# Gate and up products of a mixture of experts: eight of 512 columns, then eight of 256, in place of eight pairs

## The chip, the cores and the metric

The kernel runs on one core of one Trainium2 chip. The metric is the time of one execution on the device in microseconds (us), the median of several runs. A core has five engines that work side by side: TensorE (PE) multiplies matrices, VectorE (DVE) and ScalarE (ACT) work elementwise, GpSimd (POOL) here issues gathers and scatters, SyncE (SP) issues DMA transfers. TensorE loads a stationary operand of up to 128 x 128 (the "weights" of a product, a row PEld LDWEIGHTS in the profile) and streams a moving operand of up to 512 columns past it (a row PE MATMUL); the result goes to PSUM, where further products may be added.

## The reference

One layer of a bidirectional encoder over 2,048 tokens of 1,024 channels: a mixer stage (long convolution, neighbourhood attention, pooling), and behind it a mixture of 16 experts, each of which takes the 256 tokens that score highest for it. The change lies in the experts:

```python
def expert_choice_moe(h, w_router, w_gate, w_up, w_down):
    ...
    aff = jax.nn.softmax(h.astype(F32) @ w_router.astype(F32), axis=-1)
    gate, idx = lax.top_k(aff.transpose(0, 2, 1), cap)
    xs = jax.vmap(lambda hb, ib: hb[ib])(h, idx)
    a = jnp.einsum('becd,edf->becf', xs, w_gate)
    b = jnp.einsum('becd,edf->becf', xs, w_up)
    y = jnp.einsum('becf,efd->becd', jax.nn.silu(a) * b, w_down)
    y = y * gate.astype(y.dtype)[..., None]
    ...
```

Each expert has 1,024 x 2,048 weights for gate and for up and 2,048 x 1,024 for down, in float32.

## The kernel before

Products are made in a rounded float32 format (fp32r). To keep the precision, each operand is split into a high part, rounded, and a low part, the rest. `split` (L210 to L213) does it: ScalarE casts the high part (L212), VectorE subtracts it from the original (L213). A product of two split operands is then three products: high by high, high by low, low by high.

For an expert, `lookahead` gathers its 256 tokens (two gathers of 128 rows, tiles mo_xg, L1210), transposes them on TensorE (L1226, sixteen transposes into banks tp) and splits them into the tile mo_xx: eight slices d of 128 channels, and in each the high parts of 256 tokens beside their low parts, 512 columns in one row. It runs for the next expert in the middle of the present one (f = 3). VectorE also copies the gate's values out of the gathered rows (L1230, tile mo_gt) and builds the next indices from sums over mo_oh (L1193).

`experts` runs over 16 experts. The gate and up stage has eight steps f of 256 hidden channels, and in each a block for gate and one for up. A block loads 1 MB of weights (SP, mo_raw), splits it into mo_wh and mo_wl (three buffers each), and multiplies for two halves m of 128 hidden channels and eight slices d. For each d there is a pair: the high weights by all 512 columns of the tokens, high and low at once (L1257, tile mo_wh, 512 columns), and the low weights by the high tokens alone (L1259, tile mo_wl, 256 columns), which is added to the second half of the bank. ScalarE copies that half out (L1261), VectorE adds the other (L1262), and Silu and a product (L1265, L1266) and a split make mo_hh and mo_hl. There are 16 blocks of 32 products in an expert, 8 pairs for each m. Behind them come the down products, 192 for an expert, all of 512 columns, by `mm3` (L228, L229, L230).

The same `mm3` makes the products of the earlier stages that are cited later: the projection (tiles w_h, w_l, hT_h, hT_l, of 512 columns, and of 256 for the values) and the filter's transforms (t, d2p, of 256 columns).

A scheduler of the framework sets the order of each engine's instructions from the dependencies and an estimate of times when the program is built; within its rules the loops' order is kept for products that add to one bank. TensorE, VectorE and ScalarE each work through their list in order.

Of the kernel before, what the change touches and what calls it, by code (L numbers as in the profile page):

```python
# [183 lines left out]
class Trunk:  # L184
# [8 lines left out]
    def sb(self, pool, shape, tag, dt=F, bufs=None):  # L193
        kw = {} if bufs is None else {"bufs": bufs}
        return pool.tile(list(shape), dt, tag=tag, name=self.name(tag), **kw)
# [949 lines left out]
    def experts(self, pool):  # L1145
# [20 lines left out]
        def weights(src):  # L1166
            raw = sb(list(src.shape), "mo_raw", F, 3)
            nc.sync.dma_start(raw, src)
            h = sb(list(src.shape), "mo_wh", R, 3)
            l = sb(list(src.shape), "mo_wl", R, 3)  # L1170
            self.split(h, l, raw)
            return h, l
# [42 lines left out]
        def lookahead(e):  # L1215

            idx, xg = tokens(e)
            gate = sb([128, 2], "mo_gt", F, 2)
            xx = sb([128, 8, 2, 256], "mo_xx", R, 2)
            xh, xl = xx[:, :, 0], xx[:, :, 1]  # L1220
            for h in range(2):
                for q in range(2):
                    pt = self.bank("tp", (128, 4, 128))
                    for d in range(4):
                        dd = q * 4 + d
                        nc.tensor.transpose(pt[:, d, :], xg[h][:, dd * 128:(dd + 1) * 128], self.ident)  # L1226
                    sl = (slice(None), slice(q * 4, q * 4 + 4), slice(h * 128, h * 128 + 128))
                    self.split(xh[sl], xl[sl], pt)
                    self.first = nc.cur_bb.bb.instructions[-1]
                nc.vector.tensor_copy(gate[:, h:h + 1], xg[h][:, D + e:D + e + 1])  # L1230
            return idx, gate, xx
# [6 lines left out]
        for e in range(NE):  # L1238
            idx, gate, xx = nxt
            hh = sb([128, 16, 256], "mo_hh", R, 1)  # L1240
            hl = sb([128, 16, 256], "mo_hl", R, 1)
            for f in range(8):
                if e == 0 and f == 1:
                    late.close()
                    late.enter_context(self.tc.issue_after(first))
                if e == 1 and f == 0:
                    late.close()
                acc = []
                for src in (wg, wu):
                    w, wlo = weights(src[e, :, :, f * 256:f * 256 + 256])  # L1250


                    pt = self.bank("mm", (128, 2, 2, 256))
                    for m in range(2):
                        ms = slice(m * 128, m * 128 + 128)
                        for d in range(8):
                            nc.tensor.matmul(pt[:, m].rearrange("p k t -> p (k t)"), lhsT=w[:, d, ms],  # L1257
                                             rhs=xx[:, d].rearrange("p k t -> p (k t)"), start=d == 0, stop=False)
                            nc.tensor.matmul(pt[:, m, 1], lhsT=wlo[:, d, ms], rhs=xx[:, d, 0], start=False, stop=d == 7)  # L1259
                    a = sb([128, 2, 256], "mo_s", F, 3)  # L1260
                    nc.scalar.activation(a, pt[:, :, 1], AF.Copy)  # L1261
                    nc.vector.tensor_tensor(a, a, pt[:, :, 0], op=OP.add)  # L1262
                    acc.append(a)
                s = acc[0]
                nc.scalar.activation(s, s, AF.Silu)  # L1265
                nc.vector.tensor_tensor(s, s, acc[1], op=OP.mult)  # L1266
                self.split(hh[:, f * 2:f * 2 + 2], hl[:, f * 2:f * 2 + 2], s)
                if f == 3 and e + 1 < NE:
                    nxt = lookahead(e + 1)
            pair = [self.bank("mm", (128, 2, 512)) for h in range(2)]  # L1270
            po = [[pair[h][:, n] for n in range(2)] for h in range(2)]
            for u in range(8):
                w, wlo = weights(wd[e, :, u * 2:u * 2 + 2, :])
                for h in range(2):
                    for n in range(2):
                        for d in range(2):
                            dd = u * 2 + d
                            ts = slice(h * 128, h * 128 + 128)
                            ns = slice(n * 512, n * 512 + 512)
                            self.mm3(po[h][n], hh[:, dd, ts], hl[:, dd, ts], w[:, d, ns], wlo[:, d, ns], dd == 0, dd == 15)  # L1280
            last = e == NE - 1
            if last:
                self.final_all(pool, gf, out)
            for h in range(2):
                off = bass.IndirectOffsetOnAxis(ap=idx[:, h:h + 1].bitcast(U32), axis=0)
                y = sb([128, D], "mo_y", F, 2)
                if not last:
                    for n in range(2):
                        nc.scalar.activation(y[:, n * 512:n * 512 + 512], po[h][n], AF.Copy, scale=gate[:, h:h + 1])  # L1289
                    nc.gpsimd.indirect_dma_start(out=self.Acc, out_offset=off, in_=y, in_offset=None, compute_op=OP.add)  # L1290
                else:
                    xa = sb([128, D], "mo_xa", F, 2)
                    nc.gpsimd.indirect_dma_start(out=xa, out_offset=None, in_=self.Acc, in_offset=off)
                    for n in range(2):
                        ns = slice(n * 512, n * 512 + 512)
                        nc.vector.scalar_tensor_tensor(xa[:, ns], po[h][n], gate[:, h:h + 1], xa[:, ns],
                                                       op0=OP.mult, op1=OP.add)
                    self.final_norm(pool, y, xa, gf)
                    nc.gpsimd.indirect_dma_start(out=out, out_offset=off, in_=y, in_offset=None)
# [198 lines left out]
```

## Time and profile before

| | us |
|---|---|
| median of 3 runs | 3329.43 |
| lowest and highest run | 3318.08, 3336.1 |
| the profiled execution | 3334.13 |
| its span, first to last instruction | 3332.3 |
| TensorE, products | 3187.5 (96% of the span) |
| VectorE | 1968.4 (59%) |
| ScalarE | 1543.7 (46%) |
| GpSimd | 369.2 (11%) |

Busy time is the time in which at least one instruction of an engine runs. Products on TensorE overlap: the next starts while the one before drains, so the recorded duration of one is longer than the step to the next. The time that a stream of products takes is read from their starts. The experts run from 1147.9 us to the end, 2,184 of the 3,332 us.

A row of grouped instructions gives line, engine, operation, written tile <- read tiles, shapes and count, then busy time and mean duration in ns, then idle time of the engine just before them and who ended it. A row of the timeline gives start, duration, engine, line and operation, and in brackets the idle time before it with its releaser.

### The profile page before, as it was taken

Reading aid. Unit: us, or ns where it says so; the run is one execution under the profiler, and the core shown is the slowest. Engines: PE = TensorE matmul, PEld = TensorE weight load, DVE = VectorE, ACT = ScalarE, POOL = GpSimd, SP = SyncE. Lnnn points to the kernel's source line nnn. Section 1 sums busy time; section 2 is a strip of 40 time slices with the busy share of each in tenths; the row PEclk is TensorE's granted clock in tenths of the full one; section 3 lists DMA queues with packets and bytes.
Section 4 is the critical chain, followed back from the end, with each engine's and each line's share of the span. In section 5 each row is a group of like instructions: output and inputs, shape, how many; then the busy total and the mean of one; then the engine's idle time right before and its main releaser. Section 6 shows DMA issues by size and latency. Waiting matters only on the chain.

```text
span 3332.3 us, 44701 instructions
## 1 busy us (share of the span) xinstructions
PE 3187.5 (96%) x17646; PEld 2685.8 (81%) x17646; DVE 1968.4 (59%) x2684; ACT 1543.7 (46%) x2068; POOL 369.2 (11%) x472
## 2 busy tenths in 40 slices
PE   7999996998999499999999999999999999999998
PEld 5878885776788388888888888888888888888886
DVE  5244485445676775665655756657566566565665
ACT  4243332556432354454554545545445455454464
POOL 2222122212111000000000000000000000000012
PEclk9999998999899699999999999999999999999999
DMA  9557898567454366566676666766666667666596
GB/s 287 185 180 255 266 337 233 175 213 205 140 170 144 123 202 202 197 208 203 202 207 194 206 202 202 208 204 195 209 196 209 204 195 215 195 195 202 194 303 227
DMA packets 431144, 690.22 MB, mean 207 GB/s; under 512 B 28034, under 2 KB 325746, under 8 KB 430678
## 3 DMA queue, kind: packets, MB, share of 16 engines
q1 hardware_dynamic: 370326, 534.99, 50.6%
q0 software_dynamic: 31472, 107.09, 11.0%
q10 hardware_dynamic: 29136, 45.29, 3.9%
q8 instruction: 139, 2.28, 0.3%
q14 instruction: 71, 0.58, 0.1%
HBM read 578.58 MB, written 119.03 MB: 209 GB/s over the span
## 4 chain that ended last, share of the span: by engine, by line
PE 87%; DMA 6%; issue 2%; DVE 2%; ACT 1%; POOL 1%; SPq 1%; POOLq 0%; ACTq 0%; DVEq 0%
PE mm L1257 27%; PE mm L1259 14%; PE mm L228 11%; PE mm L229 11%; PE mm L230 11%; PE mm L217 3%; PE o L217 1%; PE tp L217 1%; PE s L217 1%; PE tp L1226 1%; DMA at_t<-Ce 1%; DMA wo_raw<-in_w_out 1%; DMA mo_xg<-Hr,mo_ix 1%; DMA x<-in_x 1%; DMA at_k<-KD 0%
## 5 line engine op out<-in xcount | busy, mean ns | idle before, releaser
L1257 PE MATMUL mm<-mo_xx,mo_wh 128*128 128x512 f32 x4096 | 1442.7, 397 | 0.8 <-DVE mo_xx L213 0.6
L213 DVE TENSOR_TENSOR mo_wl<-mo_raw,mo_wh 128x2048 fp32r<-128x2048 f32 x384 | 879.8, 2291 | 757.5 <-ACT mo_wh L212 757.3
L1259 PE MATMUL mm<-mo_xx,mo_wl 128*128 128x256 f32 x4096 | 1148.8, 281 | 0.0
L212 ACT ACTIVATE mo_wh<-mo_raw 128x2048 fp32r<-128x2048 f32 x384 | 735.8, 1917 | 713.4 <-PE mm L230 317.6
L1257 PEld LDWEIGHTS mm<-mo_xx,mo_wh 128*128 128x128 f32 x4096 | 769.6, 188 | 182.9 <-DVE mo_xx L213 1.0
L1259 PEld LDWEIGHTS mm<-mo_xx,mo_wl 128*128 128x128 f32 x4096 | 774.3, 189 | 0.7
L229 PE MATMUL mm<-mo_wl,mo_hh 128*128 128x512 f32 x1024 | 398.6, 389 | 0.0
L228 PE MATMUL mm<-mo_wh,mo_hh 128*128 128x512 f32 x1024 | 398.0, 389 | 0.0
L230 PE MATMUL mm<-mo_wh,mo_hl 128*128 128x512 f32 x1024 | 396.2, 389 | 0.0
L1290 POOL DMA_INDIRECT Acc<-mo_y,mo_ix x30 | 71.8, 2394 | 1386.6 <-ACT mo_y L1289 1272.5
L228 PEld LDWEIGHTS mm<-mo_wh,mo_hh 128*128 128x128 f32 x1024 | 192.2, 188 | 40.2
L230 PEld LDWEIGHTS mm<-mo_wh,mo_hl 128*128 128x128 f32 x1024 | 192.2, 188 | 40.0
L229 PEld LDWEIGHTS mm<-mo_wl,mo_hh 128*128 128x128 f32 x1024 | 192.2, 188 | 39.6
L1262 DVE TENSOR_TENSOR mo_s<-mo_s,mm 128x512 f32<-128x512 f32 x256 | 174.2, 680 | 0.0
L1265 ACT ACTIVATE mo_s<-mo_s 128x512 f32<-128x512 f32 x128 | 80.7, 630 | 194.7 <-DVE mo_s L1262 194.7
L228 PE MATMUL mm<-hT_h,w_h 128*128 128x512 f32 x384 | 155.8, 411 | 6.0 <-ACT hT_h L212 6.0
L229 PE MATMUL mm<-hT_l,w_h 128*128 128x512 f32 x384 | 154.9, 404 | 0.0
L230 PE MATMUL mm<-hT_h,w_l 128*128 128x512 f32 x384 | 154.1, 403 | 0.0
L1261 ACT ACTIVATE mo_s<-mm 128x512 f32<-128x512 f32 x256 | 147.8, 577 | 0.0
L212 ACT ACTIVATE mo_hh<-mo_s 128x512 fp32r<-128x512 f32 x128 | 79.7, 623 | 74.5 <-DVE mo_s L1266 74.5
L816 ACT ACTIVATE at_s<-at_s,at_min 128x360 f32<-128x360 f32 (+5 forms) x128 | 76.5, 598 | 72.0 <-DVE at_min L812 67.8
L228 PE MATMUL mm<-wo_h,mx_h 128*128 128x512 f32 x256 | 104.2, 407 | 4.0 <-DVE wo_x L1026 3.6
(325 smaller groups left out, 3878.0 us busy)
## 6 DMA issues: line engine op xcount, KB each, us to landing
mo_raw<-in_w_gate SPq DMA_DIRECT2D x128, 1024.0 KB, 11.4
mo_raw<-in_w_up SPq DMA_DIRECT2D x128, 1024.0 KB, 5.3
mo_raw<-in_w_down SPq DMA_DIRECT2D x128, 1024.0 KB, 4.8
w_r<-c_w_in_t SPq DMA_DIRECT2D x60, 256.0 KB, 8.3
x<-in_x SPq DMA_DIRECT2D x24, 512.0 KB, 4.3
Ud<-e ACTq DMA_DIRECT2D x32, 256.0 KB, 6.8
Hd<-t ACTq DMA_DIRECT2D x32, 256.0 KB, 5.5
t<-Hd SPq DMA_DIRECT2D x16, 512.0 KB, 7.3
```

Of the source, the lines that this page charges most:

```text
L212: self.nc.scalar.activation(hi, src, AF.Copy)
L213: self.nc.vector.tensor_tensor(lo, src, hi.bitcast(F), op=OP.subtract)
L217: ins = op(*args, **kw).ins
L228: mm(out, lhsT=lh, rhs=rh, start=start, stop=False)
L229: mm(out, lhsT=lh, rhs=rl, start=False, stop=False)
L230: mm(out, lhsT=ll, rhs=rh, start=False, stop=stop)
L816: nc.scalar.activation(s[:, 0:nk], s[:, 0:nk], AF.Exp, bias=mins[:, y:y + 1], scale=-1.0, accum_out=w.sums[:, col:col + 1])
L1257: nc.tensor.matmul(pt[:, m].rearrange("p k t -> p (k t)"), lhsT=w[:, d, ms], rhs=xx[:, d].rearrange("p k t -> p (k t)"), start=d == 0, sto ...
L1259: nc.tensor.matmul(pt[:, m, 1], lhsT=wlo[:, d, ms], rhs=xx[:, d, 0], start=False, stop=d == 7)
L1261: nc.scalar.activation(a, pt[:, :, 1], AF.Copy)
L1262: nc.vector.tensor_tensor(a, a, pt[:, :, 0], op=OP.add)
L1265: nc.scalar.activation(s, s, AF.Silu)
```

## The change

In the gate and up block the loop over the eight slices d is split in two: for each half m, all eight products with the high weights come first, and all eight with the low weights behind them. The products, their operands and their sums into the bank are the same; the start and stop marks stay on the first and on the last.

```diff
                         for d in range(8):
                             nc.tensor.matmul(pt[:, m].rearrange("p k t -> p (k t)"), lhsT=w[:, d, ms],
                                              rhs=xx[:, d].rearrange("p k t -> p (k t)"), start=d == 0, stop=False)
+                        for d in range(8):
                             nc.tensor.matmul(pt[:, m, 1], lhsT=wlo[:, d, ms], rhs=xx[:, d, 0], start=False, stop=d == 7)
```

From the added line on, the lines of the changed kernel count one higher: L1259 becomes L1260, L1262 becomes L1263, L1266 becomes L1267.

TensorE in block 10 of the first expert, around the second eight transposes of the look-ahead (tp, from mo_xg); mm_11173 is the block's bank. Before:

```order
L1257 MATMUL mm_11173<-mo_xx_10626,mo_wh_11169 128x512
L1259 MATMUL mm_11173<-mo_xx_10626,mo_wl_11170 128x256
L1257 MATMUL mm_11173<-mo_xx_10626,mo_wh_11169 128x512
L1259 MATMUL mm_11173<-mo_xx_10626,mo_wl_11170 128x256
L1226 MATMUL tp_11064<-ident,mo_xg_2296_11045 128x128 x4
L1226 MATMUL tp_11071<-ident,mo_xg_2296_11045 128x128 x4
L1257 MATMUL mm_11173<-mo_xx_10626,mo_wh_11169 128x512
L1259 MATMUL mm_11173<-mo_xx_10626,mo_wl_11170 128x256
```

Now:

```order
L1257 MATMUL mm_11173<-mo_xx_10626,mo_wh_11169 128x512 x8
L1260 MATMUL mm_11173<-mo_xx_10626,mo_wl_11170 128x256 x8
L1257 MATMUL mm_11173<-mo_xx_10626,mo_wh_11169 128x512 x7
L1226 MATMUL tp_11064<-ident,mo_xg_2296_11045 128x128 x4
L1226 MATMUL tp_11071<-ident,mo_xg_2296_11045 128x128 x4
L1257 MATMUL mm_11173<-mo_xx_10626,mo_wh_11169 128x512
L1260 MATMUL mm_11173<-mo_xx_10626,mo_wl_11170 128x256 x8
```

The pairs are gone, and the transposes stand behind 23 products of the block, where they stood behind 28. The first eight, in block 9, stand behind 10 where they stood behind 15.

VectorE in the same look-ahead, from the sum of block 7 (mm_10971) to the splits into mo_xx. Before:

```order
L1262 TENSOR_TENSOR mo_s_11004<-mo_s_11004,mm_10971 128x512
L1193 TENSOR_TENSOR mo_oh_12035<-mo_oh_12035 128x2048
L1230 COPY mo_gt_11047<-mo_xg_2295_11043 128x1
L1230 COPY mo_gt_11047<-mo_xg_2296_11045 128x1
L1266 TENSOR_TENSOR mo_s_10962<-mo_s_10962,mo_s_11004 128x512
L213 TENSOR_TENSOR mo_wl_11212<-mo_raw_11209,mo_wh_11211 128x2048
L1193 TENSOR_TENSOR mo_oh_12035<-mo_oh_12035 128x1024
L1262 TENSOR_TENSOR mo_s_11118<-mo_s_11118,mm_11085 128x512
L213 TENSOR_TENSOR mo_hl_10658<-mo_s_10962,mo_hh_10657 128x512
L213 TENSOR_TENSOR mo_xx_11048<-tp_11049,mo_xx_11048 128x4x128
L213 TENSOR_TENSOR mo_xx_11048<-tp_11056,mo_xx_11048 128x4x128
```

Now:

```order
L1263 TENSOR_TENSOR mo_s_11004<-mo_s_11004,mm_10971 128x512
L1230 COPY mo_gt_11047<-mo_xg_2295_11043 128x1
L1230 COPY mo_gt_11047<-mo_xg_2296_11045 128x1
L1193 TENSOR_TENSOR mo_oh_12035<-mo_oh_12035 128x2048
L1267 TENSOR_TENSOR mo_s_10962<-mo_s_10962,mo_s_11004 128x512
L213 TENSOR_TENSOR mo_wl_11212<-mo_raw_11209,mo_wh_11211 128x2048
L1263 TENSOR_TENSOR mo_s_11118<-mo_s_11118,mm_11085 128x512
L1193 TENSOR_TENSOR mo_oh_12035<-mo_oh_12035 128x1024
L213 TENSOR_TENSOR mo_xx_11048<-tp_11049,mo_xx_11048 128x4x128
L213 TENSOR_TENSOR mo_xx_11048<-tp_11056,mo_xx_11048 128x4x128
L213 TENSOR_TENSOR mo_hl_10658<-mo_s_10962,mo_hh_10657 128x512
```

The two copies of the gate, which wait for the gathers, have moved ahead of the widest sum over mo_oh, and the split into mo_hl has moved behind the two into mo_xx. Beside this some down products near the end of an expert have changed places among themselves, and in the last expert some of SP's loads of weights stand ahead of stores of the output.

## Rows read from the trace of the kernel before

**Rows 1.** Groups of instructions, whole span: line, engine, count | busy, mean ns | idle

```profile
L1257 PE MATMUL mm<-mo_xx,mo_wh 128*128 128x512 f32 x4096 | 1442.7, 397 | 0.8 <-DVE mo_xx L213 0.6 <-DVE mo_s L1262 0.2
L1259 PE MATMUL mm<-mo_xx,mo_wl 128*128 128x256 f32 x4096 | 1148.8, 281 | 0.0
...
L1259 PEld LDWEIGHTS mm<-mo_xx,mo_wl 128*128 128x128 f32 x4096 | 774.3, 189 | 0.7
```

**Rows 2.** Busy time by stretch: experts 3 and 13; last the clock, DMA share, GB/s

```profile
1554.40:1689.50 135.10, 135.10 (x725) 116.10 (x724) 83.09 (x86) 67.38 (x64) 6.99 (x5) 1.00 0.65 203
2905.60:3045.80 140.20, 137.45 (x726) 117.55 (x726) 82.95 (x86) 67.41 (x64) 8.51 (x5) 0.99 0.63 196
```

**Rows 3.** L1257 in three stretches: count, durations in ns, first and last start

```profile
L1257 PE MATMUL mm<-mo_xx,mo_wh x111: 389/398/403, 1554.4 to 1593.3; 128*128 128x512 f32 x111
L1257 PE MATMUL mm<-mo_xx,mo_wh x82: 391/391/475, 1617.5 to 1645.6; 128*128 128x512 f32 x82
L1257 PE MATMUL mm<-mo_xx,mo_wh x256: 389/398/504, 3181.4 to 3272.0; 128*128 128x512 f32 x128
```

**Rows 4.** Timeline of TensorE in filter and projection, ends of runs of one width

```profile
88.52 0.28 PE L228 MATMUL mm<-w_h,hT_h 128*128 128x256 f32 x1
...
89.47 0.28 PE L230 MATMUL mm<-w_h,hT_l 128*128 128x256 f32 x1
...
218.67 0.28 PE L229 MATMUL fl<-t,d2p 128*128 128x256 f32 x1
...
219.85 0.39 PE L229 MATMUL mm<-hT_l,w_h 128*128 128x512 f32 x1
...
221.71 0.39 PE L228 MATMUL mm<-hT_h,w_h 128*128 128x512 f32 x1
...
365.65 0.40 PE L230 MATMUL mm<-hT_h,w_l 128*128 128x512 f32 x1
...
367.75 0.39 PE L230 MATMUL mm<-hT_h,w_l 128*128 128x512 f32 x1
```

**Rows 5.** TensorE into the down products (experts 2 and 14), and settled (expert 3)

```profile
1510.85 0.39 PE L228 MATMUL mm<-mo_wh,mo_hh 128*128 128x512 f32 x1
...
1512.70 0.39 PE L230 MATMUL mm<-mo_wh,mo_hl 128*128 128x512 f32 x1
...
L228 PE MATMUL mm<-mo_wh,mo_hh x61: 389/389/389, 1648.0 to 1688.8; 128*128 128x512 f32 x61
...
3137.90 0.40 PE L228 MATMUL mm<-mo_wh,mo_hh 128*128 128x512 f32 x1
...
3139.73 0.39 PE L230 MATMUL mm<-mo_wh,mo_hl 128*128 128x512 f32 x1
```

**Rows 6.** Timeline of the look-ahead in expert 3, TensorE's gate and up left out

```profile
1606.14 1.21 DVE L1193 TENSOR_TENSOR mo_oh<-mo_oh 128x2048 bf16<-128x2048 bf16 x1
1607.27 0.14 DVE L1230 COPY mo_gt<-mo_xg 128x1 f32<-128x1 f32 x1
...
1608.03 1.03 PE L1226 MATMUL tp<-ident,mo_xg 128*128 128x128 f32 x8
1608.44 0.15 DVE L1230 COPY mo_gt<-mo_xg 128x1 f32<-128x1 f32 x1 [1.02 <-DMA mo_xg<-Hr,mo_ix]
1608.51 0.68 DVE L1266 TENSOR_TENSOR mo_s<-mo_s,mo_s 128x512 f32<-128x512 f32 x1
...
1613.11 1.28 DVE L213 TENSOR_TENSOR mo_xx<-tp,mo_xx 128x512 fp32r<-128x512 f32 x2
...
1616.66 1.03 PE L1226 MATMUL tp<-ident,mo_xg 128*128 128x128 f32 x8
```

**Rows 7.** Timeline of the look-ahead in expert 13

```profile
2965.39 0.15 DVE L1230 COPY mo_gt<-mo_xg 128x1 f32<-128x1 f32 x1 [6.79 <-DMA mo_xg<-Hr,mo_ix]
...
2970.81 1.97 PE L1226 MATMUL tp<-ident,mo_xg 128*128 128x128 f32 x8 [2.75 <-DVE mo_xx L213]
```

## The prediction

> **What bounds the kernel now.** I read the groups of instructions first, with shapes kept apart. The two gate and up products are the largest: 4,096 of 512 columns (L1257) and 4,096 of 256 (L1259), with 0.8 us of idle time before all the first and none before the second [rows 1]. So in this stage TensorE waits for nothing: no product waits for its weights, although VectorE makes the low half, which L1259 needs, last. The granted clock over a whole expert is 1.00 [rows 2], its upper level, 2.4 GHz. What counts is therefore not the recorded duration of a product (397 and 281 ns), in which neighbours overlap, but the step from one start to the next. For that I took first and last starts over long stretches.
>
> The step is not one number. In the first nine of expert 3's sixteen blocks (a block is one gate or up slab of 32 products, 16 pairs), 111 starts of L1257 lie between 1554.4 and 1593.3 us: 38.9 / 110 = 353.6 ns for a pair. In its last blocks 82 starts lie between 1617.5 and 1645.6: 28.1 / 81 = 346.9 ns [rows 3]. Same instructions, same clock, same tiles; what lies between is the look-ahead, whose transposes break the stream. TensorE's stream has more than one steady rhythm and keeps the one it fell into. Experts 1 to 12 show the split of expert 3 (nine blocks and seven), expert 0 is nearly all of the quick kind, and experts 13 to 15 nearly all of the slow kind (expert 15: 90.6 / 255 = 355.3 ns with one break in it [rows 3]). That gives 12 x 9 x 16 + 3 x 256 = 2,496 slow pairs and 12 x 7 x 16 + 256 = 1,600 quick ones: a mean of 351.0 ns for a pair now.
>
> **The change part by part.** Nothing is added or taken away: 4,096 products of each kind, each with its own weight load, the same casts, evictions, loads. The multiplications are the same, so there is no saving to be had from work; there is only what the order does to the steps, to the waits, and to the instructions that the scheduler puts elsewhere.
>
> *The steps.* Seven of eight products of 512 columns now stand ahead of another of 512, and seven of eight of 256 ahead of another of 256. Both kinds of run are in the trace elsewhere, as the same fp32r products with 128 x 128 weights.
>
> For 256 behind 256: in the filter stage ten start from 218.67 to 219.85, 118.0 ns each, between products of 512 on both sides; in the projection eight steps from 88.52 to 89.47 give 118.8 [rows 4]. I take 118.3.
>
> For 512 behind 512 the trace has three answers. Right behind that run of 256 columns, eight take 219.85 to 221.71: 232.5 ns each [rows 4]. Deep in a projection run, nine take 365.65 to 367.75: 233.3 [rows 4]. Into the down products, behind the last gate and up pair, the first eight take 1510.85 to 1512.70: 231.3; but once that run has settled, 61 starts of every third product lie between 1648.0 and 1688.8, 40.8 / 60 / 3 = 226.7 ns, and when expert 14 goes into its down products, from the slow rhythm, it settles almost at once (3137.90 to 3139.73, eight steps of 228.8) [rows 5]. After the change a run of 512 is only eight long and begins behind a run of 256. The nearest rows are the two that are the first eight behind a narrower product, 232.5 and 231.3: I take 232.
>
> The pair then costs 232 + 118.3 = 350.3 ns against 351.0, and 4,096 x -0.7 ns = -2.9 us. The ends: with the quickest eight seen, 228.8 + 118.0 = 346.8, so -4.2 x 4,096 = -17 us; with runs that lock at 226.7 from the first product, 344.7, so -26 us; with the projection's 233.3 and 118.8, 352.1, so +4.5 us.
>
> Here a rule can be weighed against a row. A weight load is recorded with 189 ns [rows 1], longer than the 118 ns step of a 256-column product; today each such product has a 512 on either side, and from now on seven of eight have not. The Trainium skill, "TensorE: Matmul & The Clock Gate", section "LDWEIGHTS (loading the stationary operand)", puts a load at its columns over 1.2 GHz, which for 128 columns is an estimate of 107 ns. By that a load still fits under a product of 256 columns and the sum stays as it is; by the recorded 189 it would not, and the third rival would hold. The 118 ns steps of rows 4 agree with the page.
>
> *The waits.* The low half of the weights is needed later: the first L1259 of a slab stood one product behind the first L1257 and now stands eight behind it, 7 x 232 = 1.6 us. Since no idle time stands before L1259 [rows 1], this gives nothing; it is slack. The high half is read to the end 8 x 118 ns earlier, so ScalarE's cast into the next free buffer may start 0.9 us sooner; it waits for TensorE and not the other way round, so that is worth nothing either. The PSUM bank is complete at the same product as before.
>
> *What the scheduler moved.* In the look-ahead the first eight transposes stand ten products into block 9 where they stood fifteen, which is 8 x 232 + 2 x 118 = 2.1 us into it, against 7 x 347 + 232 = 2.7: they come 0.6 us sooner. The second eight stand 23 products into block 10 (8 x 232 + 8 x 118 + 7 x 232 = 4.4 us) where they stood 28 (14 x 350 = 4.9): 0.5 us sooner. On VectorE the two copies of the gate, which wait for the gathers, now stand ahead of the 1.21 us sum over mo_oh instead of behind it. What is queued behind them is that sum, L1266, a low half, L1262, and the splits into mo_xx that free the banks for the second transposes. In expert 3 the second gather was there at 1608.44, after a wait of 1.02 us on VectorE. From 1608.51 to 1613.11, 4.60 us, VectorE then did L1266, the low half, a step of the sum, L1262 and a split into mo_hl, and after them the two splits into mo_xx in 1.28. Now the 1.21 us go ahead of that, and the mo_hl split, which has gone behind, I leave in as a bound: 1608.44 + 0.15 + 1.21 + 4.60 + 1.28 = 1615.7 at the latest. The second transposes came at 1616.66 and will come near 1616.2 [rows 6]. Cover: 0.5 us or more, where it was 2.3; they don't wait and this part costs nothing. The first transposes came at 1608.03, and at 1607.27 the first gather was there, for the copy had no wait [rows 6]; 0.6 us sooner is 1607.4, still behind it. If the cover goes, each microsecond costs one in each expert, 15 in all.
>
> The move of a few down products by some places, and that of SP's loads of the last expert past some stores of the output, touches no engine that is waited for: TensorE has no idle time there. The start of expert 0 has the same columns at the same low clock.
>
> **The sum.** -2.9 us for the steps, nothing for the rest. The profiled execution took 3334.1 us (span 3332.3), so 3331.2; it lies 4.7 above the median of the runs shown, 3329.4, from which the same sum gives 3326.5. I forecast 3327, no change that can be told: a measurement of this kernel can tell about 0.5% from no change, which is 16.6 us (3312.8 and 3346.1).
>
> **The rivals.**
> *The runs lock.* Runs of one width settle into the quick rhythm, as the down products do, because the stream no longer changes width at each product. For it: 226.7 ns there, and the 346.9 of the quick pairs shows that gate and up can shed 7 ns too. Against it: the projection, whose weights are stationary as here, stays at 233.3 through long runs, and eight products are hardly longer than the transient into the down stage. It gives -17 to -26 us: 3303 to 3312.
> *The gather comes late.* Expert 13 shows what it costs: there VectorE waited 6.79 us for the second gather, TensorE stood idle 2.75 us for the splits before the second transposes, and the expert took 140.2 us at a mean clock of 0.99 where expert 3 took 135.1 at 1.00 [rows 2, 7]. With the smaller cover and the copies further ahead, gathers that come over 0.5 us later than in expert 3 would stall. At 5.1 us each, four experts more (20 us) decide for slower: some 3350. Against it: of the fifteen look-aheads only this one did it.
> *The loads show.* If the 189 ns of a load can't be hidden under a run of 256 columns, 3,584 products take 71 ns more: +250 us, 3580. Rows 4 speak plainly against it.
> That the order isn't changed on the chip is no rival: TensorE runs its products as they are listed.
>
> **How the numbers follow.** Forecast (pair between 347 and 353 ns, no new stall) 0.74; locked runs 0.20, all of it faster by over 0.5%; late gathers 0.05 and visible loads 0.01, both slower. The range takes in the locked runs and the highest of the runs shown with the dear end, 3336 + 4.5: 3304 to 3341.
>
> **What would show it.** In the changed profile, starts of L1257 in its runs near 232 ns apart and L1260 near 118; no idle time before either; clock 1.00; an expert near 135 us, alike from one to the next. I am wrong if the 512-column runs stand at 227, if an idle time before L1226 or L1260 appears in many experts, or if experts take 131 or 140 us.

## The result, and the profile after

| | before | changed |
|---|---|---|
| median of the runs, us | 3327.1 (7 runs, 3318.1 to 3336.1) | 3348.5 (7 runs, 3341.4 to 3352.0) |
| ratio to before, 95% interval | | 1.0057 (1.0043 to 1.0072) |
| span of the profiled execution, us | 3332.3 | 3342.8 |
| of that, first gate product to the end, us | 2184.4 | 2205.5 |
| experts 1 to 12, first product to first product of the next, us | 135.1 each | 136.2 to 138.6, mean 136.6 |
| expert 13, expert 14, us | 140.1, 135.7 | 141.4, 137.5 |

The change costs 21.4 us by the medians. I had forecast no change that can be told: wrong, and the time lies above the range. The stretch from the first gate product to the end is 21.1 us longer, so all of it lies in the experts (what lies ahead of them differs from run to run and was 10.6 us shorter in the changed kernel's profiled run).

**The products themselves did what was forecast.** TensorE's timeline of the changed kernel, expert 3, runs of one width (start in us, busy us, line, count):

```profile
1549.51 1.11 PE L1260 MATMUL mm<-mo_xx,mo_wl 128*128 128x256 f32 x8
1550.46 2.00 PE L1257 MATMUL mm<-mo_xx,mo_wh 128*128 128x512 f32 x8
1552.30 0.88 PE L1260 MATMUL mm<-mo_xx,mo_wl 128*128 128x256 f32 x6
```

Eight of 256 columns take 1550.46 - 1549.51 = 0.95 us, 119 ns each; eight of 512 take 1.84, 230 ns. A pair costs 349 ns, and it does so in blocks 1 to 6 and 11 to 15 of expert 3 (counted from 0), where before it cost 353.6 in the early blocks and 346.9 in the late ones [rows 3]. The groups still show next to no waiting ahead of the products (last field: idle us before them, to set beside [rows 1]):

```profile
L1257 PE MATMUL mm<-mo_xx,mo_wh 128*128 128x512 f32 x4096 | 1034.5, 394 | 0.6 <-DVE mo_xx L213 0.6
...
L1260 PE MATMUL mm<-mo_xx,mo_wl 128*128 128x256 f32 x4096 | 576.4, 283 | 0.0
```

**The time went into the transposes of the look-ahead.** TensorE's waits ahead of L1226, of the changed kernel (what was waited for: us in total, times, longest):

```profile
PE tp L1226 <- DVE mo_xx L213: 16.2, 13, 2.1
PE tp L1226 <- DMA mo_xg<-Hr,mo_ix: 15.6, 3, 9.4
```

and of the kernel before:

```profile
PE tp L1226 <- DMA mo_xg<-Hr,mo_ix: 9.3, 1, 9.3
...
PE tp L1226 <- DVE mo_xx L213: 4.7, 2, 2.8
```

The 9.4 is expert 0's first gather and was there before. New are twelve waits of the second transposes for VectorE's splits, 0.9 to 2.1 us in each of experts 1 to 12 and 15.0 us in all (expert 13's 2.75 [rows 7] is gone in return), and two waits of the first transposes for the gather, 3.76 and 2.38 us in experts 13 and 14. A stop also drags something behind it: the eight transposes take 1.25 us after a wait where they took 1.03 [rows 6].

The look-ahead in expert 3 of the changed kernel, rows of VectorE, GpSimd and TensorE (in brackets the idle time before and what ended it), to set beside [rows 6]:

```profile
1593.46 1.92 DVE L1182 TENSOR_SCALAR mo_oh<-mo_iota,slot 128x256 bf16<-128x256 bf16 x9
1595.30 2.27 DVE L213 TENSOR_TENSOR mo_wl<-mo_raw,mo_wh 128x2048 fp32r<-128x2048 f32 x1
1597.50 0.95 DVE L1182 TENSOR_SCALAR mo_oh<-mo_iota,slot 128x256 bf16<-128x256 bf16 x4
...
1604.22 0.15 DVE L1230 COPY mo_gt<-mo_xg 128x1 f32<-128x1 f32 x1 [5.20 <-DMA mo_xg<-Hr,mo_ix]
...
1609.42 1.28 DVE L213 TENSOR_TENSOR mo_xx<-tp,mo_xx 128x512 fp32r<-128x512 f32 x2
...
1594.26 1.03 POOL L1210 DMA_INDIRECT mo_xg<-Hr,mo_ix  x1 [36.08 <-DVE mo_ix L1204]
1595.59 2.82 POOL L1210 DMA_INDIRECT mo_xg<-Hr,mo_ix  x1 [0.30 <-issue]
...
1610.17 1.25 PE L1226 MATMUL tp<-ident,mo_xg 128*128 128x128 f32 x8 [0.99 <-DVE mo_xx L213]
```

and what stood there in the kernel before:

```profile
1600.72 2.70 DVE L1182 TENSOR_SCALAR mo_oh<-mo_iota,slot 128x256 bf16<-128x256 bf16 x13
1603.34 2.28 DVE L213 TENSOR_TENSOR mo_wl<-mo_raw,mo_wh 128x2048 fp32r<-128x2048 f32 x1
...
1601.52 1.03 POOL L1210 DMA_INDIRECT mo_xg<-Hr,mo_ix  x1 [35.71 <-DVE mo_ix L1204]
1602.85 1.09 POOL L1210 DMA_INDIRECT mo_xg<-Hr,mo_ix  x1 [0.30 <-issue]
```

Read them in order. The masks (L1182) stood thirteen in a row and the low split of block 10's gate weights (L213, 128x2048) behind them; it began 0.49 us after GpSimd began the second gather's issue. Now the split stands behind nine masks and begins 0.29 us ahead of that issue. The issue then takes 2.82 us in place of 1.09 and ends 0.84 us after the split. The rows come 1604.22 - 1595.59 = 8.6 us after the issue began, where it was 5.6. VectorE, which works in order, stands 5.20 us at the second gate copy (L1230; before 1.02 [rows 6]), and all that is queued behind it is late: the sum, L1267, a low half, L1263, and the splits into mo_xx that free the banks for the second transposes. TensorE stands 0.99 us.

What makes the rows late has two parts. The DMA queues show the second (packets, MB, share of the 16 engines; q0 is GpSimd's queue with the gathers, q1 SyncE's with the weights), changed kernel, 1598.50 to 1601.50 and then 1601.50 to 1604.50, and SyncE's issue:

```profile
q1 hardware_dynamic: 797, 0.82, 89.4%
...
q0 software_dynamic: 144, 0.53, 45.5%
q1 hardware_dynamic: 243, 0.23, 23.4%
...
1597.60 0.37 SPq L1168 DMA_DIRECT2D mo_raw<-in_w_up  x1
```

The kernel before, 1603.90 to 1606.90, and SyncE's issue:

```profile
q0 software_dynamic: 218, 0.82, 86.8%
q1 hardware_dynamic: 5, 0.01, 0.7%
...
1605.64 0.37 SPq L1168 DMA_DIRECT2D mo_raw<-in_w_up  x1
```

The end of the split sets a buffer of raw weights free, and SyncE at once issues the next load of 1 MB into it. Before, that was 1.7 us after the second gather's issue had ended (1603.94): the gather went first. Now the held issue ends at 1598.41, 0.8 us *after* the load was issued, and for three microseconds the DMA engines move nothing but weights. The gather's 144 packets come behind them.

### The profile page after: what moved, and what is told of

It reads as the page before. It is cut to its first block, busy times and chain, and to the rows that moved or that the text cites. A ratio compares the mean times of both kernels' runs of the same rounds, so it can differ in the third digit from the quotient of the medians.

```text
span 3342.8 us, 44668 instructions
## 1 busy us (share of the span) xinstructions
PE 3183.8 (95%) x17646; PEld 2690.7 (80%) x17646; DVE 1966.0 (59%) x2684; ACT 1540.4 (46%) x2068; POOL 377.7 (11%) x472
## 3 DMA queue, kind: packets, MB, share of 16 engines
q8 instruction: 139, 2.28, 0.3%
## 4 chain that ended last, share of the span: by engine, by line
PE 68%; issue 17%; DMA 9%; DVE 4%; ACT 1%; POOL 1%; SPq 1%; POOLq 0%; ACTq 0%; DVEq 0%
PE mm L1257 15%; PE mm L228 11%; PE mm L229 11%; PE mm L230 11%; PE mm L1260 8%; DMA mo_xg<-Hr,mo_ix 4%; PE mm L217 3%; PE o L217 1%; PE tp L217 1%; PE s L217 1%; DVE mo_wl L213 1%; DMA at_t<-Ce 1%; PE tp L1226 1%; DVE mo_oh L1193 1%; DMA wo_raw<-in_w_out 1%
## 5 line engine op out<-in xcount | busy, mean ns | idle before, releaser
L213 DVE TENSOR_TENSOR mo_wl<-mo_raw,mo_wh 128x2048 fp32r<-128x2048 f32 x384 | 879.3, 2290 | 717.3 <-ACT mo_wh L212 717.3
L1257 PE MATMUL mm<-mo_xx,mo_wh 128*128 128x512 f32 x4096 | 1034.5, 394 | 0.6 <-DVE mo_xx L213 0.6
L1257 PEld LDWEIGHTS mm<-mo_xx,mo_wh 128*128 128x128 f32 x4096 | 740.7, 190 | 134.2 <-DVE mo_xx L213 1.0
L1260 PEld LDWEIGHTS mm<-mo_xx,mo_wl 128*128 128x128 f32 x4096 | 561.2, 191 | 39.4
L1260 PE MATMUL mm<-mo_xx,mo_wl 128*128 128x256 f32 x4096 | 576.4, 283 | 0.0
L1291 POOL DMA_INDIRECT Acc<-mo_y,mo_ix x30 | 57.0, 1900 | 1394.3 <-ACT mo_y L1290 1279.2
L1263 DVE TENSOR_TENSOR mo_s<-mo_s,mm 128x512 f32<-128x512 f32 x256 | 173.9, 679 | 0.0
L1262 ACT ACTIVATE mo_s<-mm 128x512 f32<-128x512 f32 x256 | 148.2, 579 | 0.0
L1210 POOL DMA_INDIRECT mo_xg<-Hr,mo_ix x32 | 60.3, 1885 | 614.3 <-DVE mo_ix L1204 572.4
L213 DVE TENSOR_TENSOR w_l<-w_r,w_h 128x512 fp32r<-128x512 f32 x80 | 60.5, 767 | 79.9 <-ACT w_h L212 79.6
```

Of the source, the lines that this page charges most:

```text
L213: self.nc.vector.tensor_tensor(lo, src, hi.bitcast(F), op=OP.subtract)
L1210: nc.gpsimd.indirect_dma_start(out=g, out_offset=None, in_=self.Hr, in_offset=bass.IndirectOffsetOnAxis(ap=idx[:, h:h + 1].bitcast(U32), a ...
```

## The experiments

My theory when I began: the moved split holds GpSimd's issue, the rows come late, VectorE stands at the gate copy, the second transposes wait. The rivals: (A) the order of the products itself makes the transposes wait; (B) the wider runs cost time elsewhere. Later ones asked what of the hold does the harm.

**e1: the changed kernel, the split put back behind all masks.**

```diff
-                    w, wlo = weights(src[e, :, :, f * 256:f * 256 + 256])
+                    with contextlib.ExitStack() as held:
+                        if f == 5 and src is wg and e + 1 < NE:
+                            held.enter_context(self.tc.issue_after(self.plus))
+                        w, wlo = weights(src[e, :, :, f * 256:f * 256 + 256])
...
+                    if f == 3 and src is wu:
+                        self.plus = nc.cur_bb.bb.instructions[-1]
```

> The changed kernel, whole, with one edit: the low split of block 10's gate weights (L213, 128x2048, 2.28 us on VectorE) is queued behind the addition of block 7, so VectorE runs all thirteen masks (L1182) first and the split starts some 3 us later than in the changed kernel. Matmuls are those of the changed kernel. Theory (the moved split holds GpSimd's second gather issue): the second gather is issued in about 1.1 us instead of 2.8, lands 5.5 to 6 us after its issue instead of 8.7, the second gate copy waits about 1 us or less, the second transposes wait nothing, block 10 falls back from 490 to 630 ns a pair to about 400, and the time is the changed kernel's less some 21 us and more of the steps' gain: 3317 to 3327, 0 to 10 us below the kernel before. Rival A (the eight-and-eight order of TensorE itself makes the second transposes wait, since they come up sooner against VectorE's queue): the waits stay and the time is 3340 to 3350. Rival B (the wider runs cost the time elsewhere, by the clock or the steps): also 3340 or more, without the waits.

Measured: 3319.3 us, ratio 0.9977 (0.9964 to 0.9989) to the kernel before. GpSimd, VectorE and TensorE in expert 3:

```profile
1598.28 1.09 POOL L1210 DMA_INDIRECT mo_xg<-Hr,mo_ix  x1 [0.30 <-issue]
...
1603.72 0.15 DVE L1230 COPY mo_gt<-mo_xg 128x1 f32<-128x1 f32 x1 [0.28 <-DMA mo_xg<-Hr,mo_ix]
...
1611.70 0.60 PE L1226 MATMUL tp<-ident,mo_xg 128*128 128x128 f32 x4
```

No wait at the transposes in any expert but expert 0, whose 9.3 us for the gather and 1.9 for the splits were there before. Experts 1 to 14 take 91.31 us each for gate and up and 43.55 for the down products; windows of experts 3 and 13 (to set beside [rows 2]):

```profile
1550.40:1685.26 134.86, 134.86 (x726) 116.55 (x725) 83.14 (x86) 66.74 (x64) 5.98 (x5) 1.00 0.66 203
2899.00:3033.86 134.86, 134.86 (x726) 116.54 (x725) 83.09 (x86) 66.75 (x64) 5.68 (x5) 1.00 0.65 203
```

The same products, still eight and eight, take 29 us less. B falls. But more than the split has moved: TensorE runs the last four of the second transposes four products later than in the changed kernel, and VectorE does the widest sum over mo_oh and L1267 ahead of the gate copies again. So this run alone neither puts the loss down to the split nor settles A; e3, e5 and e8 do that. This version beats both kernels. From the first gate product to the end it takes 2173.8 us: against it the changed kernel loses 31.7 (21.1 in experts 1 to 12, 6.5 and 2.6 in 13 and 14, 1.6 in 0 and 15) and the kernel before 10.6 (3.2 in experts 1 to 12, 5.3 in 13, 2.2 in the rest).

**e2 and e3: the new order around the transposes alone, and everywhere but there.** Blocks 8 to 11 belong to f = 4 and 5.

```diff
+                        hi = lambda d: ...  # the product of 512 columns
+                        lo = lambda d: ...  # the product of 256 columns
+                        for d in range(8):
+                            hi(d)
+                            if not (f in (4, 5)):
+                                lo(d)
+                        for d in range(8):
+                            if f in (4, 5):
+                                lo(d)
```

(e2; in e3 the condition is `f not in (4, 5)`.)

> The eight-and-eight order in blocks 8 to 11 of each expert alone (where the second transposes stand); pairs in the other twelve blocks. On VectorE block 10's split stays behind all thirteen masks, as in the kernel before. Theory: nothing is held, the second transposes wait no more than before, and the steps gain at most 1 us: 3323 to 3330, no change. Rival A (the order of the matmuls around the transposes makes the wait): the waits of 1 to 2 us are there in every expert, 3340 to 3350.

> The reverse: pairs in blocks 8 to 11, the eight-and-eight order in the other twelve. On VectorE block 10's split stands behind nine masks, ahead of the last four, as in the changed kernel. Theory: the second gather's issue is held for some 2.8 us and the second transposes wait 1 to 2 us in most experts, as in the changed kernel: 3340 to 3350. Rival A (the matmuls around the transposes): no wait, 3322 to 3328.

Measured: e3 3348.0 us, ratio 1.0061 (1.0039 to 1.0083): the whole loss, with pairs around the transposes. Its second gather's issue takes 2.82 us, the gate copy waits 5.46, the second transposes 1.42 in expert 3. That is the theory's and against A. e2: 3335.8 us, ratio 1.0023 (1.0009 to 1.0036). No issue is held (1.09 us) and no second transpose waits in experts 1 to 12, as the theory said; but 9 us above before was in neither expectation. The gate product's line after the transposes of expert 3 shows where it is, first in e2, then in the kernel before (count, ns, first and last start):

```profile
L1256 PE MATMUL mm<-mo_xx,mo_wh x62: 395/398/403, 1623.3 to 1644.8; 128*128 128x512 f32 x62
```

```profile
L1257 PE MATMUL mm<-mo_xx,mo_wh x61: 391/391/391, 1618.9 to 1639.7; 128*128 128x512 f32 x61
```

Pairs behind an eight-and-eight block run at 21.5 / 61 = 352.5 ns; pairs behind pairs with transposes in them ran at 20.8 / 60 = 346.7. 64 pairs of 6 ns are 0.4 us an expert, and the eight-and-eight blocks, at 349 and more where these pairs ran at 346.7, most of the rest of 135.70 - 135.13 = 0.57. Over twelve experts that is 6.8 of the 8.0 us by which the stretch is longer. The rhythm is inherited from what ran before, as rows 3 had hinted.

**e4: the changed kernel with the gate copies on GpSimd.** VectorE no longer stands in front of the late rows.

```diff
-                nc.vector.tensor_copy(gate[:, h:h + 1], xg[h][:, D + e:D + e + 1])
+                nc.gpsimd.tensor_copy(gate[:, h:h + 1], xg[h][:, D + e:D + e + 1])
```

> The changed kernel with the two gate copies (L1230) on GpSimd in place of VectorE. The split stays behind nine masks. Theory: the second gather's issue is still held (about 2.8 us) and its rows still land some 8.7 us after it, but VectorE no longer stands 5 to 6 us at the second gate copy, so the splits that free the transposes' banks come early and the second transposes wait little or nothing: 3317 to 3330. Rival C (the second transposes wait for the late rows themselves, and the gate copy is only a witness): they go on waiting 1 us or more in each expert, now for the transfer, 3338 to 3350.

Measured: 3327.2 us, ratio 0.9998 (0.9985 to 1.0012). TensorE no longer waits for the splits at all, and for the gathers:

```profile
PE tp L1226 <- DMA mo_xg<-Hr,mo_ix: 16.9, 4, 9.5
```

9.5 of it is expert 0; most of the rest are the first gathers ahead of experts 14 and 15, which the split holds too. So in experts 1 to 12 the second transposes did not wait for the rows but for VectorE, which stood before the gate copy. C falls.

**e5: the kernel before, with the split moved alone.**

```diff
+                    with contextlib.ExitStack() as held:
+                        if e > 1 and t >= 12:
+                            held.enter_context(self.tc.issue_after(self.low))
                         nc.vector.tensor_scalar(oh[:, t, :], iota, slot, t + 1.0, op0=OP.is_equal, op1=OP.mult)
...
+                    if f == 5 and src is wg:
+                        self.low = nc.cur_bb.bb.instructions[-1]
```

> The kernel before, pairs everywhere, with one edit: the last four of the thirteen masks (L1182) are queued behind the low split of block 10's gate weights on VectorE, so that the split stands behind nine masks, as it does in the changed kernel. No matmul moves. Theory (the moved split is the cause by itself): GpSimd's second gather issue goes from 1.09 us to some 2.8, the rows land about 8.7 us after it instead of 5.6, the second gate copy waits 4 to 6 us, the second transposes wait 0.5 to 2 us in experts 1 to 12, and the time is 3337 to 3350, 10 to 23 us above the kernel before. Rival D (it takes the new place of the split and the new order of the matmuls together, the pairs' second transposes coming 0.6 us later against the gathers): the issue is held but the second transposes wait under 0.3 us, 3325 to 3331.

Measured: 3340.6 us, ratio 1.0045 (1.0029 to 1.0061), 12.7 above before. GpSimd and VectorE in expert 3:

```profile
1597.92 2.82 POOL L1213 DMA_INDIRECT mo_xg<-Hr,mo_ix  x1 [0.30 <-issue]
...
1606.60 0.15 DVE L1233 COPY mo_gt<-mo_xg 128x1 f32<-128x1 f32 x1 [4.12 <-DMA mo_xg<-Hr,mo_ix]
```

With TensorE's order untouched, the move makes the hold and 13 of the changed kernel's 21 us, by a smaller stall than I expected: in experts 1 to 12 the second transposes wait 0.04 to 0.7 us, under 0.3 in ten of them, for in this order VectorE does the sum while it would have waited. Some 5 of the 13 us are again the rhythm: after these short waits ten of the twelve experts go on at 353 ns a pair in blocks 11 to 15 (0.5 us each), while two fall back to 346.7. D was nearly right on the size of the wait and wrong on the time.

**e6: e1 with an idle subtraction in the old place of the split.** It works on a 128x1536 tile that nothing reads.

```diff
+                    if e > 1 and t == 11:
+                        self.held.enter_context(self.tc.issue_after(nc.cur_bb.bb.instructions[-1]))
+                        nc.vector.tensor_tensor(pad, pad, pad, op=OP.subtract)
...
```

> The kernel of e1 (the split queued behind block 7's addition, nothing held) with a subtraction that computes nothing that is used, of a 128x1536 tile from itself in SBUF (three quarters of the split's size, some 1.7 us on VectorE), in the place behind nine masks that the split had in the changed kernel. Theory (a long two-operand VectorE instruction that is under way holds the gather's issue until it ends, whatever it computes): the second gather's issue takes about 2.2 us in place of 1.09, ending some 0.85 us behind the dummy's end, and its rows land 1 us or more later; the time is 0 to 10 us above that of e1, 3319 to 3330. Rival E (what holds the issue is something of the split itself, its weights' tile or its releases): the issue stays at 1.1 us, and the time at 3317 to 3322.

Measured: 3319.4 us, as e1. VectorE and GpSimd in expert 3, and the time from the second issue to the landing:

```profile
1592.73 1.74 DVE L1188 TENSOR_TENSOR mo_pad<-mo_pad 128x1536 f32<-128x1536 f32 x1
...
1593.03 2.29 POOL L1220 DMA_INDIRECT mo_xg<-Hr,mo_ix  x1 [0.30 <-issue]
...
mo_xg<-Hr,mo_ix POOLq DMA_INDIRECT x1, 5.7
```

The hold is as expected (2.29 us, ending 0.85 after the dummy), so E falls; but the rows land 5.7 us after the issue began, where e1's took 5.4. I had expected 1 us or more. My theory fell in that step: the hold alone hardly makes the rows late. What the dummy does not do, and the split does, is to set a buffer free.

**e7: the kernel before with the edit of e1.**

> The kernel before, pairs everywhere, with the edit of e1: the split queued behind block 7's addition. Theory: in experts 1 to 12 nothing was held before, so nothing changes there (91.56 us of gate and up each); the held second gathers ahead of experts 14 and 15 go, and with them some 5 us in expert 13 and 0.6 in expert 14. 3319 to 3323, 4 to 8 us below the kernel before; against e1, which has the eight-and-eight order as well, the steps alone should be 0.25 us an expert, some 4 us, so e1 should lie 3 to 5 us below this one. Rival F (the gain of e1 is all the split's, the steps bring nothing): this one is as e1, within 1.5 us.

Measured: 3325.3 us, ratio 0.9997 (0.9986 to 1.0008); no difference can be told by the times. The median lies above the 3319 to 3323 expected. By the trace expert 13 takes 135.12 us in place of 140.13, the 5 expected, and expert 14 the same 135.67, where I had expected 0.6 less; the whole stretch takes 2179.8 in place of 2184.4. Against e1, with the eight-and-eight order, it is 6.0 us longer, by the medians (taken at different times) and by the stretch alike: a little more than the 3 to 5 expected, since experts 14 and 15 run slow pairs throughout. F falls. This is the price of the change's own part, with no hold on either side.

**e8: the changed kernel, the freed load issued later.** The split stays in its new place; the load that follows it goes by ScalarE's queue, behind the casts of the first transposes.

```diff
-            nc.sync.dma_start(raw, src)
+            if behind is None:
+                nc.sync.dma_start(raw, src)
+            else:
+                with self.tc.issue_after(behind):
+                    nc.scalar.dma_start(raw, src)
...
+                    late13 = self.cast if f == 6 and src is wu and e + 1 < NE else None
+                    w, wlo = weights(src[e, :, :, f * 256:f * 256 + 256], late13)
```

> The changed kernel with one edit: the weight load that the moved split sets free (1 MB, for block 13; it is read three blocks later) is issued from ScalarE's queue behind the casts of the first transposes, instead of from SyncE's as soon as the buffer is free. VectorE's order is that of the changed kernel: the split stays behind nine masks and GpSimd's second gather issue stays held. Theory G (the hold alone is harmless, as the dummy of e6 showed; it harms because the load that the split's end releases gets to the DMA engines ahead of the held gather): the issue still takes 2.8 us, but its rows land 5.6 to 7 us after it in place of 8.6, the second transposes wait nothing in experts 1 to 12, and the time is 3317 to 3328. Rival H (the 1.7 us of the hold, and not the load, make the stall): the rows still land 8 us or more after the issue began, the second transposes wait 0.7 us or more, 3338 to 3350.

Measured: 3318.5 us, ratio 0.998 (0.9969 to 0.999). Expert 3, GpSimd, VectorE, ScalarE's queue and TensorE:

```profile
1596.52 2.82 POOL L1215 DMA_INDIRECT mo_xg<-Hr,mo_ix  x1 [0.30 <-issue]
...
1602.74 0.15 DVE L1237 COPY mo_gt<-mo_xg 128x1 f32<-128x1 f32 x1 [2.79 <-DMA mo_xg<-Hr,mo_ix]
...
1602.23 0.37 ACTq L1173 DMA_DIRECT2D mo_raw<-in_w_up  x1
...
1609.94 1.03 PE L1231 MATMUL tp<-ident,mo_xg 128*128 128x128 f32 x8
```

The issue is held as long as in the changed kernel, but the rows land 1602.74 - 1596.52 = 6.2 us after it in place of 8.6, and no second transpose waits in experts 1 to 12. The DMA queues show why: in the three microseconds that carried 797 packets of weights and none of the gather in the changed kernel (2.9 to 5.9 us after the second issue began), they carry all 144 packets of the gather and none of the weights here. From the first gate product on, TensorE, VectorE, ScalarE and GpSimd run the changed kernel's instructions one for one in its order; only the loads' issue differs. The whole loss is gone with the hold still there. G holds, H falls, and so does A: the order of the products is that of the changed kernel.

**e9: e1 with a load put ahead of the gather, and no hold.**

```diff
+                    if e > 1 and t == 10:
+                        self.held.enter_context(self.tc.issue_after(nc.cur_bb.bb.instructions[-1]))
+                        nc.vector.memset(pad[:, 0:1], 0.0)
...
+                        nc.sync.dma_start(pad, wg[0, :, 0:6, 0:256])
```

> The kernel of e1 (split behind block 7's addition, nothing held) with an additional weight load of 0.75 MB into a tile that nothing reads, issued by SyncE some 1 to 1.5 us before GpSimd ends the second gather's issue (set off by a 128x1 memset on VectorE behind eight masks). Theory G (a weight load that gets to the DMA engines first pushes the gather's rows back, with no hold at all): the issue takes 1.1 us, but the rows land 7 to 9 us after it in place of 5.4 and the second gate copy waits 1.5 to 4 us; the time is 0 to 12 us above e1, 3319 to 3332. Rival H (without the hold the rows are on time): the rows land within 6 us of the issue and the copy waits under 1 us.

Measured: 3322.0 us, ratio 0.9987 (0.9973 to 1.0001), 2.7 above e1's median; by the trace the stretch is 2.3 us longer, in experts 0 and 13 alone and nothing in 1 to 12. The second issue takes 1.01 us, and its rows land

```profile
mo_xg<-Hr,mo_ix POOLq DMA_INDIRECT x1, 7.0
```

after it began, where e1 has 5.4: a load of 0.75 MB that is issued 1.3 us before the gather's issue ends costs the rows 1.6 us with no hold. VectorE shows no wait only because the scheduler put a low half ahead of the copy here, so the wait that G named can't be seen. Together: the hold gives 0.3 to 0.8 us (e6, e8), a load ahead 1.6 (e9), and both together, where the hold lets a whole 1 MB load pass, 3.

## Why the prediction was wrong

**The steps: right in mechanism, short in size.** I priced the pair at 232 + 118.3 = 350.3 ns; it is 230 + 119 = 349. I summed -2.9 us; with no hold in either kernel the same change is worth -6.0 (e1 against e7). In experts 1 to 12 it is 135.12 - 134.86 = 0.26 each; experts 14 and 15 give more, which run slow pairs from end to end. The dear end and the locked runs both stayed out.

**The waits of the products: right.** Next to no idle time stands before L1257 and L1260 (0.6 us in all and none); the clock over experts 3 and 13 of e1 is 1.00.

**"What the scheduler moved" is the step that failed.** I took the time at which the second gather's rows land, 1608.44, from the trace of before and carried it over; only what VectorE does behind it was moved. But the rows are themselves set off by GpSimd, beside VectorE's queue, and I had not looked at what moved *there*: the low split ahead of four masks. (The listing of VectorE's order under the change begins behind these masks and doesn't show it.) In the changed kernel the rows come 8.6 us after their issue and not 5.6. The issue itself begins 0.5 us sooner in the expert, so counted from expert 3's first product (1547.70; before 1554.41) the rows come 2.5 us later; about 1.5 of that was covered and 1.0 shows. The cover was thus larger than the 0.5 I had bounded, and it did not suffice. The first transposes came where I put them (0.6 us sooner in block 9).

**The rival "The gather comes late" is what happened**, and it had the right place, the right chain (gather, VectorE, splits, second transposes) and the right pointer, expert 13. I gave it 0.05 because "of the fifteen look-aheads only this one did it". The question to ask was why that one. Its rows hold the answer: in the kernel before, the split ahead of expert 14's gather runs from 2954.52 and the second issue begins at 2955.07 and takes 2.58 us; in the look-aheads of experts 1 to 12 the split begins 0.5 to 0.6 us after the issue. Half a microsecond of order parted the two, and the change moved the order by more than that. Nor was expert 13 the only one: in expert 14 of the kernel before the second issue was held as well (2.42 us, the rows 8.26 after it began) and VectorE waited 4.40 us; only TensorE's stop was missing there. The price of a late gather I took from expert 13, 5.1 us; in twelve experts it was 1.1 to 3.5, and in expert 13 it came on top. The sign that I had named for being wrong, idle time before L1226 in many experts, is what appeared.

**What decided.** A chance of 0.06 for slower rested on a count of look-aheads, not on the margin in time between two engines.

## What to carry to other kernels

When a change moves instructions, look also at what starts and ends beside each moved one on the other engines: a margin of 0.5 us in the trace of before is a margin that a new order can spend. Follow what an instruction's end sets free, above all a buffer that a large load waits for; a load that got to the DMA engines first cost a small, urgent gather 2.4 us here (8.6 against 6.2 in e8). Where a wait sits in an in-order queue before unrelated work, as the gate copy did, moving it (e4), the order (e1) or the load (e8) each took the loss away in experts 1 to 12.

## What the runs showed of the hardware

- A gather's issue on GpSimd of 1.03 to 1.09 us took 2.82 when a 2.27 us two-operand fp32 subtraction on VectorE had begun 0.3 us before it, and 2.29 behind one of 1.74 us: each time it ended 0.84 to 0.85 us after VectorE's instruction. Beside rows of short bf16 masks it took 1.09. The Trainium skill, "SBUF — State Buffer", section "SBUF: two separate sides", says that VectorE with two SBUF inputs and a GpSimd operation that reads SBUF exclude each other for a whole instruction, whichever starts first; for GpSimd the trace agrees: 1.09 us where the issue was first by 0.49, 2.82 where the split was first by 0.29. That VectorE is held in its turn no row shows: the split took 2.28 us behind the issue and 2.27 ahead of it.
- A 1 MB load issued 0.8 us before a gather's issue ended had the DMA engines to itself for three microseconds (797 packets of q1, none of q0). With the load out of the way the held gather's packets moved in these same microseconds (e8: 144 of q0). The Trainium skill, "DMA: Bandwidth & Descriptors", section "Queues, rings and completion order", has each DMA engine take turns between its queues packet by packet. By that the two would have shared these microseconds; the rows show one behind the other. In e9 the two queues did overlap in part. What decides between the two was not tried.
- TensorE's stream of mixed widths keeps a rhythm that it inherits: the same pairs ran at 346.7 ns or 353 ns for tens of microseconds at the same clock, by what stood before them (e2, e5). Runs of eight of one width settle at 349 a pair, in the early blocks of an expert and in the late ones. What picks the rhythm is open.
